# The second ff's up projection by pairs of column groups, with three of eight k-pairs as seven-for-eight block products

## The chip, the cores and the metric

One core of a Trainium2 chip runs the whole layer as one program. The metric is the device time of one execution in microseconds (us); the median of three runs is given. The engines are PE (TensorE: matmuls and transposes, results in eight PSUM banks, called PA and PB here, four of each), DVE (VectorE), ACT (ScalarE), POOL (GpSimd) and SP (SyncE, whose queue issues most loads).

## The reference, cut to what matters

The layer is a half-step SwiGLU, a token mixing (attention and Hyena groups), and a second half-step SwiGLU, each with a norm and a modulation in front. There are 256 latent tokens, D_MODEL is 2048 and D_FF is 5632. The change lies in the second SwiGLU:

```python
def swiglu(h, w_up, w_down):
    gate, up = jnp.split(h @ w_up, 2, axis=-1)
    return (jax.nn.silu(gate) * up) @ w_down

def half_ffn(s, m, slot, g, w_up, w_down):
    h = modulate(rms_norm(s, g), chunk(m, 3 * slot), chunk(m, 3 * slot + 1))
    return s + 0.5 * chunk(m, 3 * slot + 2) * swiglu(h, w_up, w_down)

x = half_ffn(x, mod, 2, g_norm[l, 2], w_ffn2_up[l], w_ffn2_down[l])
```

All arrays are f32. Here `h` is 256 x 2048 and `w_up` 2048 x 11264.

## The kernel before

Products are done in three passes on split numbers: a number is written as hi (rounded to the type fp32r) plus lo (the remainder), and hi x hi, hi x lo and lo x hi are added up in PSUM. `split_to` makes the two: a cast on ACT (`S.copy`), and a subtraction on DVE. `weight` does the same for a loaded weight tile of 128 x 1024: the load goes out on SP's queue into one of four `raw` buffers, the cast (L236) writes one of three `whi`, the remainder (L240) one of three `wlo`.

The up projection of the second ff runs over 22 groups `g`. A group is 512 columns: 256 gate columns and the 256 up columns that belong to them. For each of eight k-pairs `kp` (two of the 16 blocks of 128 along D_MODEL) one weight tile is prepared, and `tok_mm` (L1383 to L1385) multiplies: `h` is the stationary operand (128 x 128, one token tile), the weights are the moving one (512 columns); three passes for each of two token tiles and two k-blocks, 12 matmuls per weight tile. A group accumulates in two PA banks, one for each token tile. At its end ACT takes SiLU of the gate half (L1576) and DVE multiplies it with the up half (L1577). One group later, at `kp == 2`, `turn_act` transposes the product by PE into a PB bank (four transposes of 128 x 128, L1540) and splits it into two `act` tiles (L216, L217), which the down projection takes as stationary operands.

The down projection runs over four column blocks `b` of 512, each over 22 weight tiles. At the end of a block the result is multiplied by the gate row, added to the residual stream `xt[t][b]` and stored.

SBUF tiles of most kinds come from one pool `U` of 58 buffers of 128 x 512 f32: the 16 tiles of `h`, the eight tiles of `xt`, and those of the 44 `act` tiles that don't lie in the pool `fp` (which has EXTRA of them). The order of the instructions on each engine is made by a scheduler at build time from the data's dependences and its own estimates; `then(behind, ...)` (that is, `issue_after`) forces an instruction behind another on its engine. Waits are semaphores, also built in from the dependences, so an engine executes in its order and stands still at an instruction whose operand or buffer isn't ready.

Of the kernel before, what the change touches and what calls it, by code (L numbers as in the profile page):

```python
# [11 lines left out]
F32 = mybir.dt.float32  # L12
F32R = mybir.dt.float32r
AF = mybir.ActivationFunctionType
# [4 lines left out]
P = 128  # L19
D = 2048  # L20
KT = D // P
L = 256
# [5 lines left out]
NB = 4  # L28
UPG = FF // 256
# [18 lines left out]

AWAKE2 = 8

EXTRA = 14

KV_PLAN = ((0, 0, 1), (0, 0), (0, 0, 1), (0, 0, 1), (0, 1, 0), (1, 0), (1,), (1, 1))
KV_PLAN2 = (2, 1, 2, 1, 2, 1, 2, 1)
# [8 lines left out]
def hybrid_layer_kernel(ctx: ExitStack, tc: tile.TileContext, a):  # L63
    nc = tc.nc
    V, S, G, PE = nc.vector, nc.scalar, nc.gpsimd, nc.tensor
    serial = [0]

    def T(pool, shape, tag, dt=F32, bufs=None):
        serial[0] += 1
        kw = {} if bufs is None else {"bufs": bufs}  # L70
        return pool.tile(list(shape), dt, tag=tag, name=f"{tag}_{serial[0]}", **kw)

    const = ctx.enter_context(tc.tile_pool(name="const", bufs=1))
    wp = ctx.enter_context(tc.tile_pool(name="wp", bufs=3))
    up = ctx.enter_context(tc.tile_pool(name="up", bufs=1))
    pp = ctx.enter_context(tc.tile_pool(name="pp", bufs=4, space=PSUM))

    def U(shape, dt=F32):
        return T(up, shape, "u", dt, 58)
# [7 lines left out]
    def PA(shape=(P, 512)):  # L87
        return T(pp, shape, "pa")

    def PB(shape=(P, 512)):  # L90
        return T(pp, shape, "pb")
# [564 lines left out]
    dram = ctx.enter_context(tc.tile_pool(name="dram", bufs=1, space=bass.MemoryType.DRAM))  # L656
    spec = [T(dram, (P, 2, L), f"spec{i}") for i in range(8)]
    silu_rows = T(dram, (2, KT, P), "silu_rows")
    actd = [T(dram, (P, 2, 2, L), f"act{j}", F32R) for j in range(JT)]

    def filter_spectrum():
# [137 lines left out]
    for i in range(2):  # L799
        for q in range(KT // 2):  # L800
            t = U((P, 2, L))
# [6 lines left out]
    w = {j: tuple(T(wp, (P, 4, 2, P), n, F32R, 3) for n in ("whi", "wlo")) for j in range(WAVE)}  # L808
# [28 lines left out]
    sums = PB((P, 4, 2))  # L837
    awake = keep_awake(AWAKE[0])
    step, acc, summed = None, None, []
# [4 lines left out]
    for n, t in enumerate(xs[0] + xs[1]):  # L844
        i, sq = n // 8, U((P, 2, L))
# [5 lines left out]
        if n in (7, 14):  # L851
            sq = acc
# [11 lines left out]
        summed, last = [], awake  # L864
# [55 lines left out]
    made = then(roots[-1], first_hi, 0, head)  # L920
    for j in range(WAVE):
        made = then(made, first_hi, j, head) if j else made
# [3 lines left out]
    with tc.issue_after(scaled.ins):  # L926
        copied, turned_, bank = then(spread_last, ada_col, 0)
# [26 lines left out]
    with tc.issue_after(mm.ins), tc.issue_after(scaled.ins), tc.issue_after(shifted.ins):  # L954
        copied, mm, _ = ada_col(1)
# [4 lines left out]
    with tc.issue_after(shifted.ins), tc.issue_after(lo_last.ins):  # L960
        for j in range(2):
            first_lo(j, second)
        made = first_hi(2, second)
# [569 lines left out]
        shape = (P, 2, L)  # L1533
        return U(shape, F32R) if n >= EXTRA else T(fp, shape, "act", F32R, EXTRA)

    def turn_act(g, at):
        pt = PB((P, 2, L))
        for f in range(2):
            for t in range(2):
                PE.transpose(pt[:, f, t * P : (t + 1) * P], at[:, t, f * P : (f + 1) * P], ident)  # L1540
        acts.append(split_to(pt, act_tile(2 * g), act_tile(2 * g + 1)))

    prev = None
    for g in range(UPG):
        ps = [PA(), PA()]
        behind = None
        if g == 0:
            for t in range(2):
                for k in range(4):
                    tok_mm(ps, [h[k][:, s, :] for s in range(2)], ws[k], k == 0, False, (t,))  # L1550
                if t == 0:
                    pt = turned(xn)
                    for d in range(4):
                        hi, lo = mod2(d, pt[:, d, :], h[d][:, :, P:L])
                        behind = behind or (lo, hi)
            rest_h(1)
        for kp in range(8):
            if g == 0 and kp < 2:
                continue
            if g == 0 and kp == 2:  # L1560
                pieces = ws[4:6]
            else:
                late = dict(zip(("behind", "behind_hi"), behind)) if g == 0 and kp < 6 else {}
                whi, wlo = weight(a["w_up2"][g, kp], (P, 2, 512), **late)
                pieces = [(whi[:, k2, :], wlo[:, k2, :]) for k2 in range(2)]
            for k2 in range(2):
                k = 2 * kp + k2
                tok_mm(ps, [h[k][:, s, :] for s in range(2)], pieces[k2], k == 0, k == KT - 1)
            if g == 0 and kp in (2, 4):
                rest_h(kp // 2 + 1)  # L1570
            if kp == 2 and prev:
                turn_act(*prev)
        at = U((P, 2, L))
        for t in range(2):
            sg = tmp2((P, L))
            S.activation(sg, ps[t][:, 0:L], AF.Silu)  # L1576
            V.tensor_mul(at[:, t, :], ps[t][:, L : 2 * L], sg)  # L1577
        prev = (g, at)
    h = None
    for b in range(NB):  # L1580
        ps = [PA(), PA()]
        for fq in range(UPG):
            whi, wlo = weight(a["w_dn2"][b, fq], (P, 2, 512))
            if b == 0 and fq == UPG // 2:
                grow = gate_row(1)
            if b == 0 and fq == 2:
                turn_act(*prev)
            for t, f in ((0, 0), (1, 0), (0, 1), (1, 1)) if fq < UPG - 1 else ((0, 0), (0, 1), (1, 0), (1, 1)):
                tok_mm(ps, [t_[:, f, :] for t_ in acts[fq]], (whi[:, f, :], wlo[:, f, :]), fq + f == 0, fq == UPG - 1 and f == 1, (t,))
        for t in range(2):  # L1590
            o = tmp2((P, 512))
            V.tensor_mul(o, ps[t], grow[b])
            V.tensor_add(xt[t][b], xt[t][b], o)
            nc.sync.dma_start(a["out"][t, :, b * 512 : (b + 1) * 512], xt[t][b])
# [48 lines left out]
def _prepare(i):  # L1643
    i = {k: np.asarray(v) for k, v in i.items()}
    c_ = np.ascontiguousarray

    def pcol(v):
        return c_(v.reshape(-1, P).T)

    def pair(w, ncol):  # L1650
        return c_(w.reshape(4, 4, P, 2, ncol, P).transpose(4, 0, 2, 1, 3, 5))

    def wide(w):
        n = w.shape[1] // 256
        return c_(w.reshape(4, 4, P, n, 256).transpose(3, 0, 2, 1, 4)).reshape(n, 4, P, 4, 2, P)

    def down(w):
        return c_(w.reshape(JT // GRP, GRP, P, 8, 256).transpose(0, 3, 2, 1, 4)).reshape(JT // GRP, 8, P, GRP, 2, P)

    def cols(w):  # L1660
        return c_(w.reshape(8, 2, P, 512).transpose(0, 2, 1, 3))

    d = _constants()
    xc = np.concatenate([i["x"][0], i["ctx"][0]], axis=0)
    d["xT"] = c_(xc.reshape(2, L, KT // 2, 2, P).transpose(0, 2, 4, 3, 1))
    cc = np.stack([i["c"][0], i["c_ctx"]])
    d["crow"] = c_(cc)
    cs = cc.reshape(2, KT, P).transpose(2, 1, 0).reshape(P, 2, KT)
    wa = i["w_ada"][0]
    d["w_adaT"] = c_(wa.T).reshape(9 * KT, P, D)  # L1670
    blocks = [np.concatenate([wa[:, o + b * P : o + (b + 1) * P] for o in (D, 0)], axis=1) for b in range(KT)]
    d["w_ada1"] = np.stack([w.reshape(2, 8, P, 2 * P).transpose(0, 2, 1, 3) for w in blocks])
    gn = i["g_norm"][0].reshape(3, KT, P).transpose(2, 0, 1)
    d["cond"] = np.concatenate([pcol(i["b_ada"][0]).reshape(P, 9, KT), gn, cs], axis=1)
    w = pair(i["w_ffn1_up"][0], JT)
    d["w_up1"] = c_(w[:WAVE])
    w = w[WAVE:].reshape(JT - WAVE, 4, P, 2, 4, P)
    d["w_up1q"] = c_(w[:, :, :, :, [0, 2, 3, 1], :])
    d["w_dn1"] = down(i["w_ffn1_down"][0])
    w = i["w_ffn2_up"][0].reshape(8, 2, P, 2, UPG, 256)  # L1680
    d["w_up2"] = c_(w.transpose(4, 0, 2, 1, 3, 5)).reshape(UPG, 8, P, 2, 512)
    d["w_dn2"] = c_(i["w_ffn2_down"][0].reshape(UPG, 2, P, NB, 512).transpose(3, 0, 2, 1, 4))
    wi = i["w_in"][0]
    d["w_kv"] = cols(c_(wi[:, 1024:1536]))
    d["w_q"] = np.stack([cols(c_(wi[:, 0:512])), cols(c_(wi[:, 512:1024]))])
    d["w_hy"] = pair(np.concatenate([wi[:, 3584:4608], wi[:, 2560:3584]], axis=1), CT)
    d["w_x0"] = wide(c_(wi[:, 1536:2560]))
    d["w_o"] = np.stack([cols(c_(i["w_out"][0][:, b * 512 : (b + 1) * 512])) for b in range(NB)])

    def eo(v):  # L1690
        return np.concatenate([v[0::2], v[1::2]])

    d["qkg"] = np.stack([eo(i["q_norm"][0]), eo(i["k_norm"][0])])
    d["convw"] = c_(i["conv_w"][0].reshape(3, 3 * CT, P).transpose(2, 0, 1))
    d["convb"] = pcol(i["conv_b"][0])
    d["hyb"] = pcol(i["hy_bias"][0])
    d["gout"] = pcol(i["g_out"][0])
    w1, w2, w3, d["flt_w4"] = (c_(i[f"flt_w{n}"][0]) for n in (1, 2, 3, 4))
    head = np.zeros((P, 4, 64), np.float32)
    head[0:33, 0], head[0:64, 1], head[0:64, 2], head[0:64, 3] = w1, w2, w3, w3  # L1700
    vec = np.stack([i["flt_b1"][0], i["flt_b2"][0], i["flt_b3"][0], i["flt_freq"][0]], axis=1)
    d["flt_head"] = np.concatenate([head.reshape(P, 256), np.concatenate([vec, vec]), d.pop("tneg")], axis=1)
    d["flt_decay"] = c_(i["flt_decay"][0].reshape(1, 2 * HW))
    return d
# [19 lines left out]
```

## Time and profile before

| what | value |
|---|---|
| median of three runs | 2610.24 us (2609.64 to 2611.66) |
| the profiled execution's own time | 2610.55 us |
| its span in the profile | 2608.7 us |
| granted TensorE clock, mean | 0.998 |
| PE busy | 2587.4 us, 99% of the span, 14480 matmuls and transposes |
| DVE busy | 1895.7 us, 73%, 3051 instructions |
| ACT busy | 1103.9 us, 42%, 1543 instructions |
| HBM read, written | 544.05 MB, 38.57 MB |

The span goes from the first to the last instruction that the profiler saw; the execution's time has some 2 us more around it. "Busy" is the sum of the instructions' times on an engine. A wait is listed with what released it. The second ff's up projection begins at about 1870 us of the span and ends at about 2365 us; the down projection follows until the end.

### The profile page before, as it was taken

The page shows a single profiled execution, that of the slowest core. Times are in us where ns is not written, and L with a number is a line of the kernel's source. Part 1 is how long each engine was busy: PE and PEld are TensorE (multiplying, and loading weights), DVE is VectorE, ACT ScalarE, POOL GpSimd, SP SyncE. Part 2 cuts the span into 40 slices and gives each one's busy share as a digit, 9 for nine tenths or more (in the row PEclk, how much of TensorE's full clock was granted, in tenths as well). Part 3 has the DMA queues.
Part 4 walks back from the last instruction along what each step waited for, and adds up shares of the span by engine and source line. Part 5 has one row for each costly group of instructions (what it writes and reads, how often), then busy time and mean ns, then how long its engine had stood idle before and what let it go on. Part 6 is the DMA issues. An engine that isn't in the chain of part 4 may idle for free.

```text
span 2608.7 us, 37979 instructions
## 1 busy us (share of the span) xinstructions
PE 2587.4 (99%) x14480; PEld 2226.6 (85%) x14480; DVE 1895.7 (73%) x3051; ACT 1103.9 (42%) x1543; POOL 298.6 (11%) x475
## 2 busy tenths in 40 slices
PE   8999999999999999999999999999999999999999
PEld 5678999999999998888888988888788888888887
DVE  6776888888888887778988786888755454544444
ACT  5344444444444442112211565466544444444333
POOL 1122222222222223310010000000000000000000
PEclk9999999999999999999999999999999999999999
DMA  9987889889889889996897566335556665656664
GB/s 368 358 283 215 250 244 251 243 242 255 249 251 249 241 241 356 395 324 210 295 330 229 168 194 187 109 128 175 170 187 192 187 192 187 191 188 209 201 202 155
DMA packets 194275, 606.63 MB, mean 233 GB/s; under 512 B 22923, under 2 KB 25964, under 8 KB 189740
## 3 DMA queue, kind: packets, MB, share of 16 engines
q1 hardware_dynamic: 134396, 482.37, 56.0%
q0 software_dynamic: 59504, 121.70, 18.3%
q8 instruction: 113, 1.85, 0.3%
q14 instruction: 70, 0.57, 0.1%
q10 hardware_dynamic: 192, 0.13, 0.0%
HBM read 544.05 MB, written 38.57 MB: 223 GB/s over the span
## 4 chain that ended last, share of the span: by engine, by line
PE 95%; DMA 2%; DVE 1%; issue 1%; ACT 0%; SPq 0%; POOL 0%; POOLq 0%; DVEq 0%; ACTq 0%
PE pa L1384 10%; PE pa L1383 10%; PE pa L1385 10%; PE pb L247 9%; PE pb L248 9%; PE pb L249 9%; PE pa L247 9%; PE pa L248 9%; PE pa L249 9%; PE pa L255 3%; PE pa L257 2%; PE pa L1097 1%; PE pa L1098 1%; PE pa L1096 1%; DMA wrow<-in_w_ada_dram 1%
## 5 line engine op out<-in xcount | busy, mean ns | idle before, releaser
L240 DVE TENSOR_TENSOR wlo<-raw,whi 128x1024 fp32r<-128x1024 f32 x483 | 590.4, 1223 | 470.8 <-ACT whi L236 469.6
L236 ACT CAST whi<-raw 128x1024 fp32r<-128x1024 f32 x483 | 508.3, 1053 | 876.8 <-PE pa L1385 413.3
L1383 PE MATMUL pa<-whi,u 128*128 128x512 f32 x1060 | 413.9, 391 | 0.0
L1384 PE MATMUL pa<-wlo,u 128*128 128x512 f32 x1060 | 412.8, 390 | 0.2 <-DVE wlo L240 0.2
L1385 PE MATMUL pa<-whi,u 128*128 128x512 f32 x1060 | 412.9, 390 | 0.0
L247 PE MATMUL pa<-u,whi 128*128 128x256 f32 (+1 forms) x912 | 307.1, 337 | 2.1 <-ACT u L894 2.1
L248 PE MATMUL pa<-u,whi 128*128 128x256 f32 (+1 forms) x912 | 304.8, 334 | 0.4 <-DVE u L899 0.4
L249 PE MATMUL pa<-u,wlo 128*128 128x256 f32 (+1 forms) x912 | 304.5, 334 | 0.0
L247 PE MATMUL pb<-u,whi 128*128 128x256 f32 (+1 forms) x904 | 300.1, 332 | 0.0
L248 PE MATMUL pb<-u,whi 128*128 128x256 f32 (+1 forms) x904 | 298.5, 330 | 0.0
L249 PE MATMUL pb<-u,wlo 128*128 128x256 f32 (+1 forms) x904 | 298.4, 330 | 0.0
L1385 PEld LDWEIGHTS pa<-whi,u 128*128 128x128 f32 x1060 | 199.0, 188 | 41.6
L1384 PEld LDWEIGHTS pa<-wlo,u 128*128 128x128 f32 x1060 | 199.1, 188 | 41.3 <-DVE wlo L240 0.6
L1383 PEld LDWEIGHTS pa<-whi,u 128*128 128x128 f32 x1060 | 199.0, 188 | 40.7
L151 DVE CUSTOM_DVE_ANT_0 adas<-adaw,crow,cond 128x1024 bf16<-128x1024 f32 x160 | 204.8, 1280 | 13.0 <-DMA adaw<-in_w_adaT_dram 11.2
L151 DVE CUSTOM_DVE_ANT_0 adas<-adaw,crow,mod 128x1024 bf16<-128x1024 f32 x160 | 204.9, 1281 | 12.1 <-DMA adaw<-in_w_adaT_dram 10.1
L459 ACT CAST bhi<-raw 128x768 fp32r<-128x768 f32 x111 | 92.5, 833 | 268.6 <-PE pb L248 133.8
L247 PEld LDWEIGHTS pa<-u,whi 128*128 128x128 f32 x912 | 173.1, 190 | 24.7 <-issue 4.9
L248 PEld LDWEIGHTS pa<-u,whi 128*128 128x128 f32 x912 | 173.5, 190 | 17.5 <-DVE u L899 1.5
L249 PEld LDWEIGHTS pa<-u,wlo 128*128 128x128 f32 x912 | 173.5, 190 | 17.1
L247 PEld LDWEIGHTS pb<-u,whi 128*128 128x128 f32 x904 | 171.8, 190 | 17.0 <-issue 1.6
L248 PEld LDWEIGHTS pb<-u,whi 128*128 128x128 f32 x904 | 171.9, 190 | 16.3 <-issue 0.9
(361 smaller groups left out, 4817.5 us busy)
## 6 DMA issues: line engine op xcount, KB each, us to landing
adaw<-in_w_adaT_dram SPq DMA_DIRECT2D x224, 512.0 KB, 5.9
raw<-in_w_dn_dram SPq DMA_DIRECT2D x182, 512.0 KB, 4.4
raw<-in_w_up_dram SPq DMA_DIRECT2D x176, 512.0 KB, 3.5
raw<-in_w_up1q_dram SPq DMA_DIRECT2D x124, 512.0 KB, 5.1
u<-act POOLq DMA_DIRECT2D x136, 256.0 KB, 10.6
wrow<-in_w_ada_dram SPq DMA_DIRECT2D x32, 1024.0 KB, 9.3
act<-sg POOLq DMA_DIRECT2D x86, 256.0 KB, 6.3
plain<-in_w_up1q_dram POOLq DMA_DIRECT2D x80, 256.0 KB, 4.6
```

The lines of the kernel that those rows point to most:

```text
L151: V.tensor_tensor_reduce(out=sc, in0=t, in1=crow[i][:, b * (D // 2) : (b + 1) * (D // 2)], scale=1.0, scalar=mcol if b else bada[:, c * KT ...
L236: S.copy(hi, raw)
L240: last_lo[0] = V.tensor_sub(lo, raw, hi.bitcast(F32))
L247: PE.matmul(ps, w[0], xx[0], start=start, stop=False)
L248: PE.matmul(ps, w[0], xx[1], start=False, stop=False)
L249: return PE.matmul(ps, w[1], xx[0], start=False, stop=stop)
L255: PE.matmul(ps, w[0], x, start=start, stop=stop)
L257: PE.matmul(ps[:, 0, :], w[1], x[:, 0, :], start=False, stop=False)
L459: return raw, hi, lo, S.copy(hi, raw[:, :, 0:3])
L1383: PE.matmul(ps[t], hi, w[0], start=start, stop=False)
L1384: PE.matmul(ps[t], hi, w[1], start=False, stop=False)
L1385: last = PE.matmul(ps[t], lo, w[0], start=False, stop=stop)
```

## The change

Groups 0 and 1 stay as they were, but for two things: at `g == 0`, `kp == 5`, the residual stream's eight tiles are stored in DRAM by POOL's queue, and at `g == 1` the sums and differences of `h`'s blocks are made for three k-pairs (`combine`). The other 20 groups are done as ten pairs `p`. A pair accumulates in four banks (one for each token tile and group). For each k-pair, `quad` prepares both groups' weights one k-pair ahead.

In pairs 1 to 9 the k-pairs 2, 4 and 6 are "summed": the 2 x 2 blocks of `h` (two token tiles, two k-blocks) times the 2 x 2 blocks of weights (two k-blocks, two groups) are done by seven products of block sums instead of eight products of blocks. `quad` then makes the sums of the weights' blocks on DVE, in place in the raw buffers, and splits them; three of the seven products go into the pair's four banks directly, four go into four extra banks (`mixed`), which `collect` adds up into SBUF after k-pair 6; `gated` adds these to the pair's banks at the end. The prepared weights lie in five unit buffers: three in the pool `wp`, two in `fp`. All casts of the quads are issued in one order on ACT, and all sums and remainders in one order on DVE (`in_turn`).

Both groups of a pair are transposed at the next pair's k-pair 1. In the down projection the two tiles of the residual stream that a block needs are loaded back by POOL's queue. The weights of groups 2 to 21 come in another layout (`w_up2p`) with the same number of bytes.

```diff
-EXTRA = 14
+EXTRA = 9
+SUMMED = (2, 4, 6)
+SUM_PAIRS = range(1, 10)
...
+    xtd = [[T(dram, (P, 512), f"xt{t}_{b}") for b in range(NB)] for t in range(2)]
...
+    def combine(kp):
+        m_, s_ = tmp2((P, 2, L)), U((P, 4, P))
+        for n in range(2):
+            V.tensor_add(m_[:, n, :], h[2 * kp + n][:, 0, :].bitcast(F32), h[2 * kp + n][:, 1, :].bitcast(F32))
+        (a11, a21), (a12, a22) = ((m_[:, n, 0:P], m_[:, n, P:L]) for n in range(2))
+        V.tensor_add(s_[:, 0, :], a21, a22)
+        V.tensor_sub(s_[:, 1, :], s_[:, 0, :], a11)
+        V.tensor_sub(s_[:, 2, :], a11, a21)
+        V.tensor_sub(s_[:, 3, :], a12, s_[:, 1, :])
+        sums[kp] = split(s_, (P, 4, P))
...
+    def unit():
+        units[0] += 1
+        pool, tag, bufs = (wp, "w", 3) if units[0] % 5 < 3 else (fp, "v", 2)
+        return tuple(T(pool, (P, 2, 512), tag + name, F32R, bufs) for name in ("hi", "lo"))
+
+    def in_turn(engine, do, *args):
+        queue[engine] = then(queue[engine], do, *args) if engine in queue else do(*args)
...
+    def quad(p, kp):
+        raw = [weight_load(a["w_up2p"][p - 1, 2 * kp + k2], (P, 2, 512)) for k2 in range(2)]
+        if not summed(p, kp):
+            made = []
+            for k2 in range(2):
+                made.append(unit())
+                cast_in_turn(made[-1][0], raw[k2])
+                rest_in_turn(made[-1][1], raw[k2], made[-1][0])
+            return made
+        (b11, b12), (b21, b22) = ((r[:, 0, :], r[:, 1, :]) for r in raw)
+        first = tuple(T(up, (P, 512), "sq", F32R, 2) for _ in range(2))
+        plain, odd, even = unit(), unit(), unit()
+        cast_in_turn(first[0], b11)
+        cast_in_turn(plain[0], raw[1])
+        rest_in_turn(first[1], b11, first[0])
+        rest_in_turn(plain[1], raw[1], plain[0])
+        in_turn("dve", V.tensor_sub, b11, b12, b11)
+        in_turn("dve", V.tensor_sub, b12, b22, b12)
+        cast_in_turn(odd[0], raw[0])
+        in_turn("dve", V.tensor_sub, b22, b22, b11)
+        in_turn("dve", V.tensor_sub, b21, b21, b22)
+        rest_in_turn(odd[1], raw[0], odd[0])
+        cast_in_turn(even[0], raw[1])
+        rest_in_turn(even[1], raw[1], even[0])
+        return plain, first, odd, even
...
+    def multiply(p, kp, w, banks, mixed):
+        ks = [[h[2 * kp + k2][:, s_, :] for s_ in range(2)] for k2 in range(2)]
+        if not summed(p, kp):
+            for k2 in range(2):
+                for n in range(2):
+                    tok_mm([banks[t, n] for t in range(2)], ks[k2], halves(w[k2], n), kp + k2 == 0, kp == 7 and k2 == 1)
+            return
...
+        for bank, x, w_, inner in ((banks[0, 0], part(ks[1], 0), halves(plain, 0), True),
+                                   (banks[0, 1], part(both, 3), halves(plain, 1), True),
+                                   (mixed[0], part(ks[0], 0), first, False),
+                                   (mixed[3], part(both, 0), halves(odd, 0), False),
+                                   (mixed[2], part(both, 2), halves(odd, 1), False),
+                                   (banks[1, 0], part(ks[1], 1), halves(even, 0), True),
+                                   (mixed[1], part(both, 1), halves(even, 1), False)):
+            tok_mm([bank], x, w_, not inner and begin, not inner and end, (0,))
+
+    def collect(mixed):
+        e11, e21, e12, e22 = (U((P, 512)) for _ in range(4))
+        u2 = tmp2((P, 512))
+        S.copy(e11, mixed[0])
+        V.tensor_add(u2, e11, mixed[1])
+        V.tensor_add(e21, u2, mixed[2])
+        V.tensor_add(e12, u2, mixed[3])
+        V.tensor_add(e22, e21, mixed[3])
+        return {(0, 0): e11, (0, 1): e12, (1, 0): e21, (1, 1): e22}
+
+    def gated(p, banks, extra):
+        for n in range(2):
+            at = U((P, 2, L))
+            for t in range(2):
+                c_ = banks[t, n]
+                if extra:
+                    V.tensor_add(extra[t, n], extra[t, n], c_)
+                    c_ = extra[t, n]
+                sg = tmp2((P, L))
+                S.activation(sg, c_[:, 0:L], AF.Silu)
+                V.tensor_mul(at[:, t, :], c_[:, L : 2 * L], sg)
+            yield 2 * p + n, at
...
-    for g in range(UPG):
+    for g in range(2):
...
+            if g == 0 and kp == 5:
+                for t in range(2):
+                    for b in range(NB):
+                        nc.gpsimd.dma_start(xtd[t][b], xt[t][b])
+            if g == 1 and kp in (3, 4, 5):
+                combine(SUMMED[kp - 3])
...
+    plan = [(p, kp) for p in range(1, UPG // 2) for kp in range(8)]
+    ahead = quad(*plan[0])
+    turns = [prev]
+    for n, (p, kp) in enumerate(plan):
+        mine, other = (PB, PA) if p % 2 else (PA, PB)
+        if kp == 0:
+            banks = {(t, n_): mine() for n_ in range(2) for t in range(2)}
+            mixed = extra = None
+        if kp == SUMMED[0] and p in SUM_PAIRS:
+            mixed = [other() for _ in range(4)]
+        w = ahead
+        if n + 1 < len(plan):
+            ahead = quad(*plan[n + 1])
+        multiply(p, kp, w, banks, mixed)
+        if kp == 1:
+            for turn_ in turns:
+                turn_act(*turn_, other)
+        if kp == SUMMED[-1] and mixed:
+            extra = collect(mixed)
+        if kp == 7:
+            turns = list(gated(p, banks, extra))
+    h = sums = None
     for b in range(NB):
         ps = [PA(), PA()]
+        for t in range(2):
+            xt[t][b] = U((P, 512))
+            nc.gpsimd.dma_start(xt[t][b], xtd[t][b])
...
             if b == 0 and fq == 2:
-                turn_act(*prev)
+                for turn_ in turns:
+                    turn_act(*turn_)
```

`cast_in_turn` is `S.copy` and `rest_in_turn` is `V.tensor_sub` (raw less hi), both through `in_turn`; `summed(p, kp)` is true for the 27 summed k-pairs; `halves(w, n)` is group `n`'s half of a unit's hi and lo, and `part(x, n)` a token tile's half of an `h` tile, or one of the four made by `combine`.

More of the change, by code (lines that the diff above doesn't have):

```diff
@@ L1534, in act_tile, with turn_act @@
         return U(shape, F32R) if n >= EXTRA else T(fp, shape, "act", F32R, EXTRA)
-    def turn_act(g, at):
-        pt = PB((P, 2, L))
+    def turn_act(g, at, bank=PB):
+        pt = bank((P, 2, L))
         for f in range(2):
@@ L1541, in turn_act @@
         acts.append(split_to(pt, act_tile(2 * g), act_tile(2 * g + 1)))
+    sums = {}
+    def combine(kp):
[8 more added lines that the diff above has]
+        sums[kp] = split(s_, (P, 4, P))
@@ new lines, in hybrid_layer_kernel, with cast_in_turn, rest_in_turn @@
+    units = [0]
+    queue = {}
+    def unit():
[4 more added lines that the diff above has]
+        queue[engine] = then(queue[engine], do, *args) if engine in queue else do(*args)
+    def cast_in_turn(hi, raw):
+        in_turn("act", S.copy, hi, raw)
+    def rest_in_turn(lo, raw, hi):
+        in_turn("dve", V.tensor_sub, lo, raw, hi.bitcast(F32))
@@ new lines, in summed @@
+    def summed(p, kp):
+        return p in SUM_PAIRS and kp in SUMMED
+    def quad(p, kp):
[23 more added lines that the diff above has]
+        return plain, first, odd, even
@@ new lines, in halves, with part @@
+    def halves(w, n):
+        return [t[:, n, :] for t in w]
+    def multiply(p, kp, w, banks, mixed):
[5 more added lines that the diff above has]
+            return
+        plain, first, odd, even = w
+        def part(x, n):
+            return [t[:, n * P : (n + 1) * P] for t in x]
+        both = [t.rearrange("p a b -> p (a b)") for t in sums[kp]]
+        begin, end = kp == SUMMED[0], kp == SUMMED[-1]
+        for bank, x, w_, inner in ((banks[0, 0], part(ks[1], 0), halves(plain, 0), True),
[6 more added lines that the diff above has]
+            tok_mm([bank], x, w_, not inner and begin, not inner and end, (0,))
@@ L1578, in hybrid_layer_kernel @@
         prev = (g, at)
-    h = None
+    plan = [(p, kp) for p in range(1, UPG // 2) for kp in range(8)]
[20 more added lines that the diff above has]
+    h = sums = None
     for b in range(NB):
         ps = [PA(), PA()]
+        for t in range(2):
+            xt[t][b] = U((P, 512))
+            nc.gpsimd.dma_start(xt[t][b], xtd[t][b])
         for fq in range(UPG):
@@ L1680, in _prepare @@
     w = i["w_ffn2_up"][0].reshape(8, 2, P, 2, UPG, 256)
-    d["w_up2"] = c_(w.transpose(4, 0, 2, 1, 3, 5)).reshape(UPG, 8, P, 2, 512)
+    d["w_up2"] = c_(w.transpose(4, 0, 2, 1, 3, 5)[:2]).reshape(2, 8, P, 2, 512)
+    w = i["w_ffn2_up"][0].reshape(KT, P, 2, UPG // 2, 2, 256)
+    d["w_up2p"] = c_(w.transpose(3, 0, 1, 4, 2, 5)[1:]).reshape(UPG // 2 - 1, KT, P, 2, 512)
     d["w_dn2"] = c_(i["w_ffn2_down"][0].reshape(UPG, 2, P, NB, 512).transpose(3, 0, 2, 1, 4))
```

## The prediction

> **What bounds the kernel now.** I read the slices of the page first, then its chain, then the stage that is edited. The page:
>
> ```profile
> PE 2587.4 (99%) x14480; PEld 2226.6 (85%) x14480; DVE 1895.7 (73%) x3051; ACT 1103.9 (42%) x1543; POOL 298.6 (11%) x475
> DVE  6776888888888887778988786888755454544444
> PEclk9999999999999999999999999999999999999999
> PE 95%; DMA 2%; DVE 1%; issue 1%; ACT 0%; SPq 0%; POOL 0%; POOLq 0%; DVEq 0%; ACTq 0%
> ```
>
> PE is busy throughout and is 95% of the chain that ended last; DVE's digits fall to 5 and 4 in the last quarter, where the second ff lies. That stage by windows (stretch, length, busy us and count of PE, PEld, DVE, ACT, POOL, then clock, DMA share, GB/s), the second row being the down projection; then the first stretch's groups by form (line, engine, shapes, count, busy us, mean ns, idle before and its releaser):
>
> ```profile
> 1900.00:2300.00 400.00, 400.00 (x1800) 330.98 (x1799) 202.48 (x198) 171.83 (x199) 0.00 (x0) 1.00 0.61 190
> 2365.00:2603.00 238.00, 238.00 (x1054) 197.05 (x1053) 113.47 (x100) 90.38 (x87) 0.00 (x0) 1.00 0.63 194
> ```
>
> ```profile
> L240 DVE TENSOR_TENSOR wlo<-raw,whi 128x1024 fp32r<-128x1024 f32 x144 | 176.4, 1225 | 190.8 <-ACT whi L236 190.8
> L236 ACT CAST whi<-raw 128x1024 fp32r<-128x1024 f32 x145 | 152.6, 1052 | 206.5 <-PE pa L1385 206.5
> L1577 DVE TENSOR_TENSOR u<-pa,sg 128x256 f32<-128x256 f32 x36 | 15.3, 424 | 7.2 <-ACT sg L1576 4.6
> L1540 PE MATMUL pb<-ident,u 128*128 128x128 f32 x72 | 10.8, 272 | 0.0
> L217 DVE TENSOR_TENSOR act<-pb,act 128x512 fp32r<-128x512 f32 x7 | 4.8, 682 | 0.0
> ```
>
> Four hundred of 400 us are PE; DVE works 202 and waits for ACT's casts, which wait for PE to free a weight buffer. So this stage is bound by the number of matmuls, and DVE has about half its time free. A matmul's record overlaps its successor's, so its price is the distance of starts:
>
> ```profile
> 1893.81 0.39 PE L1383 MATMUL pa<-whi,u 128*128 128x512 f32 x1
> ...
> 1899.93 0.39 PE L1383 MATMUL pa<-whi,u 128*128 128x512 f32 x1
> ```
>
> There are 27 starts between these two: 6.12 / 27 = 0.2267 us per matmul. The period of a group, from ACT's SiLU to the same one a group later:
>
> ```profile
> 2007.28 0.38 ACT L1576 ACTIVATE sg<-pa 128x256 f32<-128x256 f32 x1 [0.98 <-PE pa L1385]
> 2029.53 0.38 ACT L1576 ACTIVATE sg<-pa 128x256 f32<-128x256 f32 x1 [0.98 <-PE pa L1385]
> ```
>
> That is 22.25 us: 96 x 0.2267 = 21.76, and 0.49 for four transposes (0.12 each). Two groups take 44.5 us.
>
> **The change, part by part.**
>
> *Matmuls (the gain).* Call a k-pair of two column groups a quad. A plain quad is 24 matmuls (2 k-tiles x 2 groups x 2 token tiles x 3 passes), 5.44 us; a summed one has seven products of three, 21 matmuls, 4.76 us. Summed are k-pairs 2, 4, 6 of pairs 1 to 9: 27 quads, 81 matmuls of an unchanged shape: 81 x 0.2267 = 18.4 us. The transposes stay the same in number. A summed pair of groups becomes 183 x 0.2267 + 8 x 0.12 = 42.5 us of PE.
>
> *DVE (the cost that must hide).* Its ops back to back:
>
> ```profile
> 1843.84 0.75 DVE L1406 SCALAR_TENSOR_TENSOR sg<-pa,small,u 128x512 f32<-128x512 f32 x1
> 1844.62 0.69 DVE L1407 TENSOR_TENSOR u<-u,sg 128x512 f32<-128x512 f32 x1
> 1845.23 0.74 DVE L1406 SCALAR_TENSOR_TENSOR sg<-pa,small,u 128x512 f32<-128x512 f32 x1
> 1845.89 1.21 DVE L240 TENSOR_TENSOR wlo<-raw,whi 128x1024 fp32r<-128x1024 f32 x1
> 1847.02 0.68 DVE L1407 TENSOR_TENSOR u<-u,sg 128x512 f32<-128x512 f32 x1
> 1847.62 0.68 DVE L217 TENSOR_TENSOR u<-raw,u 128x512 fp32r<-128x512 f32 x1
> 1848.23 1.22 DVE L240 TENSOR_TENSOR wlo<-raw,whi 128x1024 fp32r<-128x1024 f32 x1
> ```
>
> A 512-wide op costs 0.61 from start to start (1844.62 to 1845.23, 1847.62 to 1848.23) and a 1024-wide one 1.13 (1845.89 to 1847.02). An op that needs the one just before it starts 0.12 later (1843.84 to 1844.62 is 0.78, where the same op with an independent successor takes 0.66). A summed pair of groups now holds 10 remainders of plain units and 9 of summed ones (19 x 1.13 = 21.5); 512-wide: 15 in the summed quads (one remainder and four sums each), four in collect, four adds in gated, two in the turns (25 x 0.61 = 15.3); four gate products (4 x 0.42 = 1.7); some 11 dependent steps (1.3). Sum 39.8 us under PE's 42.5: DVE goes from under half to 94%, just below PE.
>
> The Trainium skill ("VectorE: DVE Perf Modes", section "The DRAIN you can't avoid") says that after an operation the next one doesn't start until the pipe is empty, and in the same breath that one which isn't held starts earlier. The rows above are of the second sort: successors start 0.08 us before the record ends.
>
> Without that overlap the same work is 19 x 1.225 + 25 x 0.69 + 4 x 0.424 = 42.2 us, level with PE; that is a rival below.
>
> *Does each summed quad arrive in time?* Five unit buffers serve 2 + 3 units, so a summed quad is prepared while the summed quad before it and the plain one between them run (4.76 + 5.44 = 10.20 us). ACT's half-size cast and the landings:
>
> ```profile
> L216 ACT CAST u<-raw 128x512 fp32r<-128x512 f32 x6 | 3.4, 614 | 0.4 <-DMA raw<-in_w_up_dram 0.4
> raw<-in_w_up_dram SPq DMA_DIRECT2D x176, 512.0 KB, 3.5
> raw<-in_w_up1q_dram SPq DMA_DIRECT2D x124, 512.0 KB, 5.1
> adaw<-in_w_adaT_dram SPq DMA_DIRECT2D x224, 512.0 KB, 5.9
> act<-sg POOLq DMA_DIRECT2D x86, 256.0 KB, 6.3
> u<-act POOLq DMA_DIRECT2D x136, 256.0 KB, 10.6
> ```
>
> Let k-pair 2's products start at 0. The small buffer ("first") comes free after the third product, 9 x 0.2267 + about 0.2 for the tail of the record = 2.24. Then: first cast to 2.85, plain cast to 3.9, plain remainder to 5.05, two sums to 6.3, the next two sums to 7.6 beside the odd cast, odd remainder to 8.75, even remainder to 9.9. Products of k-pair 4 start at 10.2 and want plain at once, odd at 12.24, even at 13.6: 5.1, 3.5 and 3.7 us early. For k-pair 6 the raw buffers are freed at 8.75 and 9.9 and the loads land 3.5 to 4 us later, so the plain cast starts at 13.9, the odd remainder ends at 19.8 and the even one at 20.95; wanted at 22.44 and 23.8. It is about 2.7 us early, the tightest place. The plain quad between (remainders at 9.9 to 11.1 and 11.5 to 12.6) is wanted from 14.96. Casts and remainders are issued in one order per engine (in_turn), so a late sum also holds the next quad's. After k-pair 6 come three plain quads in a row, and the slack is refilled. So I take zero for these waits; the bounds are 0 (nothing in this work can shorten PE) and 0.45 us per summed quad, i.e. 12 us, by the rows 5.1 and 5.9 for a landing (1.6 to 2.4 us more, just inside the 2.7) plus a cast queued wrongly ahead (1.05). If this cover goes, PE waits in the odd or even product, and every quad behind it moves.
>
> *Collect, gate, turns.* Collect: one copy and four adds, 0.6 + 4 x 0.61 + dependent steps = 3.3 us after k-pair 6; its banks are wanted at the next pair, 5.4 us later. Gated: four adds and four products, 4.1 us on DVE, at the next pair's k-pair 0; their banks are wanted after k-pair 1, 10.9 us on. What is queued behind these on DVE and ACT is the preparation of the next pair's quads. Before, that fits:
>
> ```profile
> 2006.33 1.23 DVE L240 TENSOR_TENSOR wlo<-raw,whi 128x1024 fp32r<-128x1024 f32 x1 [1.50 <-ACT whi L236]
> 2007.70 0.42 DVE L1577 TENSOR_TENSOR u<-pa,sg 128x256 f32<-128x256 f32 x1
> 2008.38 0.42 DVE L1577 TENSOR_TENSOR u<-pa,sg 128x256 f32<-128x256 f32 x1 [0.26 <-ACT sg L1576]
> 2009.31 1.23 DVE L240 TENSOR_TENSOR wlo<-raw,whi 128x1024 fp32r<-128x1024 f32 x1 [0.51 <-ACT whi L236]
> ```
>
> The gate takes the place where it becomes ready, between remainders of weights that are wanted later. I take 0; bounds 0 to 2 us per pair (18 us), half of the 4.1 us showing.
>
> *Combine*, three times in group 1. The nearest ops by size:
>
> ```profile
> L1453 DVE TENSOR_TENSOR u<-mt,u 128x256 fp32r<-128x256 f32 x12 | 4.5, 420 | 0.6 <-ACT u L1453 0.6
> L1453 DVE TENSOR_TENSOR u<-mt,u 128x128 fp32r<-128x128 f32 x6 | 1.5, 286 | 2.2 <-ACT u L1453 2.2
> ```
>
> Two 256-wide (0.42 each), four 128-wide (0.29), one remainder 0.68: 2.7 us each, 8 us in a group of 22 us where DVE is half idle; 0, at most 8. The start of pair 1 fills units in other buffers: I allow 1 us with this (0 to 3).
>
> *The residual stream.* Eight stores of 256 KB on POOL's queue, which is idle here (0.00 in the windows), and two loads per down block of 59.5 us (238 / 4). Landing by the rows 6.3 and 10.6 us, nobody waits. The 2.1 MB go beside weight loads at 190 GB/s and 0.61 share; the casts wait for PE, not for loads, in all 206.5 us. Zero; at most 2.1 MB / 0.31 MB per us (190 / 0.61 GB/s) = 6.7 us, were all of it in the weights' way. The freed buffers are taken up: in pair 9, 16 for h, 6 for the sums, 36 - 9 = 27 act tiles, 4 of collect and 2 products make 55 of 58, so no tile should wait for a buffer.
>
> **Sum.** The profiled execution took 2610.55 us (span 2608.7): 2610.55 - 18.4 + 1 = 2593.2. The median of the runs, 2610.24, lies 0.3 lower, so 2593.
>
> **Rivals.**
>
> 1. *Partial stalls* of 0.15 to 0.45 us per summed quad, at k-pair 6, where the slack is least: 4 to 12 us come back, 2597 to 2605. For it: 94% on DVE. Against: 2.7 us of slack.
>
> 2. *The pair's end eats the gain*: gate and collect stand ahead of the next quads' casts and remainders on in-order engines, and PE waits 2.04 us at each of nine pairs (18.4 / 9). Result about 2610, no change. For it: 4.1 us of gate where 0.85 stood, and k-pair 1 wants its remainders 5.4 us after the pair's end (4.1 + 2 x 1.13 = 6.4, already 1 us late if all of it went first). Against: the order in the rows above.
>
> 3. *Slower: DVE becomes the bound.* If ops don't overlap once each is held by a wait, a pair is 42.2 us of DVE, and each summed quad has hand-offs to ACT in which DVE stands idle (0.5 us ahead of the plain remainder in my schedule, more where a raw is late). From 2.3 us of idle per pair (44.5 - 42.2) the change loses; with 3.3 us it is 9 x 1.0 = 9 us more: 2619. For it: the chain of casts and sums is serial. Against: the overlaps shown, which hold also for L217 with its cast awaited.
>
> It is also what the section "The DRAIN you can't avoid" of the Trainium skill's "VectorE: DVE Perf Modes" would come to here, its first half taken at its word.
>
> **Chances.** Forecast 0.57 (its own range 2590 to 2597); rival 1 0.14; rival 2, within 0.2% (5.2 us, about what a measurement of this kernel tells from no change) 0.14; rival 3 and other slower ones, such as landings over 8 us (3.5 + 2.7 + 2.04), 0.15. Faster is 0.57 + 0.14 = 0.71. The range 2589 to 2609 takes the first two and most of the third, about 0.8; its low end is the sum without the 1 us (2592) less 0.1% for the measurement.
>
> **What would show it.** Right: 14,399 instructions on PE; a period of 42.5 us from pair to pair; DVE about 94% busy in pairs 1 to 9, and no PE wait on a remainder. DVE's busy time grows by 27 x (5 x 0.69 + 1.225) + 18 x 2.76 + 8 = 184 us to about 2080. Wrong: PE waits listed at the odd or even products (slack mis-sized), at k-pairs 0 and 1 (pair's end), or a DVE without gaps and a pair of 44.5 us or more (DVE the bound).

## The result, and the profile after

The changed kernel takes 2625.23 us (median of four runs, 2623.91 to 2627.84) against 2610.68 us for the kernel before in the same comparison: ratio 1.0057, 95% interval 1.0040 to 1.0074. The forecast was 2593. It is some 15 us slower where 18 less were expected, so about 32 us have to be found.

The page of the changed kernel, the lines that answer to those of before:

```profile
PE 2581.5 (98%) x14399; PEld 2212.3 (84%) x14399; DVE 2054.0 (78%) x3306; ACT 1148.9 (44%) x1609; POOL 307.3 (12%) x491
DVE  6777888888888886778988786888778888874444
PE 81%; DVE 8%; DMA 7%; ACT 3%; issue 1%; ACTq 0%; SPq 0%; DVEq 0%
```

The 81 instructions are gone from PE (14480 to 14399), and yet PE holds only 81% of the chain that ended last, 95% before: DVE, DMA and ACT have come into it. The stretch from the transposes of pair 3 to those of pair 10, seven pairs long, as windows (stretch, length, busy us and count of PE, PEld, DVE, ACT, POOL, clock, DMA share, GB/s):

```profile
2022.90:2345.18 322.28, 304.88 (x1338) 244.45 (x1337) 276.25 (x335) 168.69 (x204) 1.08 (x2) 1.00 0.56 185
```

A pair takes 322.28 / 7 = 46.04 us: 42.5 were forecast, and 44.5 is two groups of before. PE is no longer full (304.88 of 322.28), nor is DVE (276.25, 86%), nor ACT, nor the DMA engines (0.56). No engine is saturated, so the loss has to lie in what waits for what. PE's stops from pair 4's second quad to the end of its summed ones, out of its timeline (L1386 to L1388 are the three passes of `tok_mm`, L1543 the transposes, L219 the remainder of a turned product; L272 is the helper that forces an order, so there the tiles tell what an operation is: `whi` and `wlo`, `vhi` and `vlo` are units, `sq` is the first block, and `raw` a sum in place):

```profile
2064.46 0.50 PE L1387 MATMUL pa<-wlo,u 128*128 128x512 f32 x1 [1.01 <-DVE wlo L272]
2069.82 1.03 PE L1543 MATMUL pb<-ident,u 128*128 128x128 f32 x8
2074.58 0.50 PE L1386 MATMUL pb<-vhi,u 128*128 128x512 f32 x1 [0.99 <-DVE u L219]
2095.41 0.49 PE L1386 MATMUL pb<-vhi,u 128*128 128x512 f32 x1 [0.38 <-ACT vhi L272]
2096.83 0.50 PE L1387 MATMUL pb<-vlo,u 128*128 128x512 f32 x1 [0.93 <-DVE vlo L272]
```

PE stops at k-pair 2's fifth product (2074.58), which waits for DVE to split the turned products and free a bank, and at k-pair 6's fourth (2095.41 and 2096.83), which waits for the odd unit's cast and remainder. Every pair from 3 to 9 shows these two, and some a stop at a plain quad (2064.46). What those waits stand on is told by the chain that ended last in this stretch (start, us, what):

```profile
2072.82 4.80 DMA raw<-in_w_up2p_dram
...
2077.69 1.06 ACT whi L272
...
2078.78 1.22 DVE wlo L272
2080.00 0.61 DVE raw L272
...
2080.64 0.70 DVE raw L272
...
2081.36 0.70 DVE raw L272
...
2082.09 0.70 DVE raw L272
...
2083.17 1.06 ACT vhi L272
...
2084.25 1.24 DVE vlo L272
2085.51 4.97 DMA raw<-in_w_up2p_dram
```

No PE stands in it. It is one round of one raw buffer: a load, the plain cast, the plain remainder, four sums in place (each waits for its predecessor), the even cast, the even remainder, and only then is the buffer free for the next load, 12.69 us later (2072.82 to 2085.51). Four raw buffers hold the loads of two quads, so a round has to serve one summed and one plain quad, 10.20 us of products.

The round begins late, too. Ahead of it, at the pair's end, the same chain lies on DVE for most of 11.8 us (2060.98 to 2072.82):

```profile
2059.58 1.05 ACT whi L272
...
2060.98 0.42 DVE u L1658
2061.41 0.60 DVE u L1654
...
2066.48 1.14 DVE wlo L272
...
2071.57 1.24 DVE vlo L272
```

These are the gate's adds (L1654) and products (L1658) among the remainders, then k-pair 2's sums and remainders; the last of them frees the buffer for the load at 2072.82.

### The profile page after: what moved, and what is told of

It is laid out like the page before. It is cut to its first block, busy times and chain, and to the rows that moved or that the text cites. A ratio compares the mean times of both kernels' runs of the same rounds, so it can differ in the third digit from the quotient of the medians.

```text
span 2624.4 us, 38215 instructions
## 1 busy us (share of the span) xinstructions
PE 2581.5 (98%) x14399; PEld 2212.3 (84%) x14399; DVE 2054.0 (78%) x3306; ACT 1148.9 (44%) x1609; POOL 307.3 (12%) x491
## 4 chain that ended last, share of the span: by engine, by line
PE 81%; DVE 8%; DMA 7%; ACT 3%; issue 1%; ACTq 0%; SPq 0%; DVEq 0%
PE pb L249 9%; PE pb L250 9%; PE pb L251 9%; PE pa L249 9%; PE pa L250 9%; PE pa L251 9%; DMA raw<-in_w_up2p_dram 5%; PE pa L1387 5%; PE pa L1388 5%; PE pa L1386 5%; PE pa L257 3%; DVE raw L272 3%; DVE wlo L272 2%; PE pa L259 2%; ACT whi L272 1%; DVE vlo L272 1%
## 5 line engine op out<-in xcount | busy, mean ns | idle before, releaser
L238 ACT CAST whi<-raw 128x1024 fp32r<-128x1024 f32 x323 | 339.9, 1053 | 649.0 <-PE pb L250 191.5
L242 DVE TENSOR_TENSOR wlo<-raw,whi 128x1024 fp32r<-128x1024 f32 x323 | 394.4, 1222 | 259.5 <-ACT whi L238 258.4
L1388 PE MATMUL pa<-whi,u 128*128 128x512 f32 x656 | 255.6, 390 | 0.0
L1387 PE MATMUL pa<-wlo,u 128*128 128x512 f32 x640 | 250.3, 391 | 4.7 <-DVE wlo L272 4.1
L1386 PE MATMUL pa<-whi,u 128*128 128x512 f32 x640 | 250.1, 392 | 3.2 <-DVE u L219 1.9
L251 PEld LDWEIGHTS pb<-u,wlo 128*128 128x128 f32 x904 | 171.9, 190 | 15.6
L464 DVE TENSOR_TENSOR blo<-raw,bhi 128x768 fp32r<-128x768 f32 x111 | 106.2, 956 | 95.5 <-ACT bhi L461 95.4
L272 ACT CAST whi<-raw 128x1024 fp32r<-128x1024 f32 x115 | 118.8, 1051 | 105.6 <-DVE raw L272 47.9
```

The costliest lines, as they stand in the source:

```text
L238: S.copy(hi, raw)
L242: last_lo[0] = V.tensor_sub(lo, raw, hi.bitcast(F32))
L251: return PE.matmul(ps, w[1], xx[0], start=False, stop=stop)
L272: return do(*args, **kw)
L464: return V.tensor_sub(lo, raw[:, :, 0:3], hi.bitcast(F32))
L1386: PE.matmul(ps[t], hi, w[0], start=start, stop=False)
```

## The experiments

Theory A: four raw buffers are too few for such a round, since a load can be asked for only when the quad two before has been prepared. Theory B: DVE's amount of work, and its hand-offs with ACT, set the pace. Theory C: the turned products' split stands in the wrong place of DVE's queue. Theory D: the structure by pairs costs by itself. Times of before in the same comparisons were 2610.7 to 2610.9 us.

**Without the sums (e1).**

```diff
-SUM_PAIRS = range(1, 10)
+SUM_PAIRS = ()
```

> SUM_PAIRS is empty, all else as in the changed kernel: pairs of groups, four banks, quads one ahead, the residual stream in DRAM; no seven-for-eight products, no sums, no collect. If the loss comes from how the summed quads are prepared (theory A, raw buffers, or B, DVE), PE goes without a stop: 2112 products again, so 2609 to 2613 us. If the pair structure itself costs (theory D: gate of four banks, two groups turned together, residual stores beside the loads), 2616 us or more.

Measured: 2610.12 us, ratio 1.0000 (0.9990 to 1.0009). Theory D falls: the four banks, the gate of four (without the adds of the sums), the two turns at once and the residual stream's way through DRAM cost nothing that can be measured. The loss is in the summed quads.

**A fifth raw buffer (e2).** `raws` counts the quads' loads; every fifth goes to a buffer in `fp`.

```diff
-EXTRA = 9
+EXTRA = 7
...
+    def quad_load(src):
+        raws[0] += 1
+        if raws[0] % 5 < 4:
+            return weight_load(src, (P, 2, 512))
+        raw = T(fp, (P, 2, 512), "more", bufs=1)
+        nc.sync.dma_start(raw, src)
+        return raw
...
-        raw = [weight_load(a["w_up2p"][p - 1, 2 * kp + k2], (P, 2, 512)) for k2 in range(2)]
+        raw = [quad_load(a["w_up2p"][p - 1, 2 * kp + k2]) for k2 in range(2)]
```

> A fifth raw buffer for the quads, in the place of two act tiles (EXTRA 7). Theory A: the round of one raw buffer (load 4.9, cast 1.06, remainder 1.22, four sums 2.85, cast 1.06, remainder 1.24 = about 12.4 us) for each 10.2 us of products is what is late; with five buffers a load is asked for one tile earlier, most of the 2.2 us of lateness goes: 2600 to 2612 us. Theory B: DVE's own work and order set the pace, a load that lands earlier changes nothing: 2622 to 2628 us.

Measured: 2592.92 us, ratio 0.9935 (0.9921 to 0.9950): below the range I gave theory A, and what the prediction had said of the change itself. The windows of the same seven pairs:

```profile
2014.05:2310.79 296.74, 296.74 (x1339) 246.15 (x1337) 276.08 (x333) 168.33 (x202) 1.08 (x2) 1.00 0.61 205
```

PE is full again, and a pair takes 42.39 us. With five buffers a round may last as long as five tiles' products in place of four, by the same count 10.20 x 5 / 4 = 12.75 us (an estimate). DVE does the same 276 us of work in less time (93%), with the same hand-offs to ACT. So neither is the bound, and theory B falls. In this stretch PE's matmuls have no wait at all. ACT's longest waits are now for the sums, which lie off PE's path; the casts that follow a load wait for PE once more, for instance the small one:

```profile
ACT sq L272 <- PE pa L1387: 5.6, 8, 0.7
```

(eight times, 5.6 us in total, in the list of waits). That is the order of things the prediction drew; in the changed kernel the same cast waits for a load:

```profile
ACT sq L272 <- DMA raw<-in_w_up2p_dram: 21.1, 19, 1.8
```

**The other half of that edit (e5).** Only EXTRA 7.

> The other half of the edit with five buffers, by itself: EXTRA 7 and four raw buffers, so that two act tiles more lie in the common pool. Theory A (the raw buffers alone): as the changed kernel, 2621 to 2629 us. If the place of the act tiles had made the gain: 2592 to 2600 us.

Measured: 2622.53 us, ratio 1.0044 (1.0029 to 1.0059). The place of the act tiles makes some 3 of the 32 us, and its interval overlaps the changed kernel's; the buffer makes the gain.

**The sums taken out of the round (e7).** This kernel leaves out the four sums of the weights' blocks, so its summed quads don't multiply what the layer asks for. In their place four subtractions of the same size on other data stand behind the quad's last remainder.

```diff
-        in_turn("dve", V.tensor_sub, b11, b12, b11)
-        in_turn("dve", V.tensor_sub, b12, b22, b12)
...
-        in_turn("dve", V.tensor_sub, b22, b22, b11)
-        in_turn("dve", V.tensor_sub, b21, b21, b22)
...
         rest_in_turn(even[1], raw[1], even[0])
+        aside = tmp2((P, 512))
+        for _ in range(4):
+            in_turn("dve", V.tensor_sub, aside, *[h[n].rearrange("p a b -> p (a b)").bitcast(F32) for n in range(2)])
```

> Four raw buffers; the four sums of each summed quad are left out, and four subtractions of the same size on other data (two h tiles into a scratch tile) are issued behind the quad's last remainder: the same number of DVE operations, none of them between a load and the raw buffer's release. Theory A: the round is 12.5 - 2.85 = 9.7 us, under 10.2: 2592 to 2605 us. Theory B (DVE's total of work): 2620 to 2628 us, as before the edit.

Measured: 2592.09 us, ratio 0.9927 (0.9910 to 0.9943), with four raw buffers and an unchanged number of DVE operations. PE has no stop in the pairs here either. The fifth buffer gave the round more time; this edit makes the round shorter (9.7 us by the sum above), and the time is the same. By itself e7 changes two things, since the odd and even casts no longer wait for sums; e2 kept those waits and lost the stops as well. Theory A holds; B is out.

**Another order, and the loads swapped (e3).**

```diff
-        raw = [weight_load(a["w_up2p"][p - 1, 2 * kp + k2], (P, 2, 512)) for k2 in range(2)]
+        raw = [None, None]
+        for k2 in (1, 0) if summed(p, kp) else (0, 1):
+            raw[k2] = weight_load(a["w_up2p"][p - 1, 2 * kp + k2], (P, 2, 512))
...
         rest_in_turn(first[1], b11, first[0])
-        rest_in_turn(plain[1], raw[1], plain[0])
         in_turn("dve", V.tensor_sub, b11, b12, b11)
         in_turn("dve", V.tensor_sub, b12, b22, b12)
+        rest_in_turn(plain[1], raw[1], plain[0])
```

> The same work in another order, four raw buffers: in a summed quad the second k-block's load goes first, and the two sums that need no remainder are made ahead of the plain remainder. Theory A: the round gets shorter by two sums and by one remainder's wait, 12.4 to about 9.9 us, below the 10.2 us of products, so the stops at k-pair 6 go (1.65 us per pair, 15 us in all): 2603 to 2613 us. Theory B (DVE's total of 39 us per pair and its hand-offs): same work, 2620 to 2628 us.

Measured: 2633.08 us, ratio 1.0081 (1.0066 to 1.0096), slower still. I had worked out its round wrongly. With the loads swapped, the first block lands last, and the whole order hangs on it, since its small cast is the first in the queue. The chain of this kernel:

```profile
2076.20 4.60 DMA raw<-in_w_up2p_dram
...
2080.88 0.63 ACT sq L272
...
2081.54 0.70 DVE sq L272
...
2088.72 4.33 DMA raw<-in_w_up2p_dram
```

The round is 12.52 us (2076.20 to 2088.72), not 9.9: what the sums no longer add behind the load, the small cast and its remainder do, and two sums stand ahead of the plain remainder, which PE wants first:

```profile
2097.12 0.50 PE L1387 MATMUL pa<-wlo,u 128*128 128x512 f32 x1 [1.17 <-DVE wlo L272]
```

The result misses both ranges and speaks neither for B nor against A; the edit didn't do what it was for.

**The order alone (e6).** The second half of that diff without the swap.

> The order of e3 without its change of the loads: the first k-block's load goes first again, and the small cast, its remainder and one sum are done while the second one still lands. Theory A: from the later landing the round is 4.9 + cast 1.06 + remainder 1.2 + two sums 1.4 + cast 1.06 + remainder 1.24 = 10.9 us in place of 12.5, near to the 10.2 us of products: most of the stops at k-pair 6 go, 2603 to 2614 us. Theory B (DVE's amount of work): 2622 to 2630 us.

Measured: 2613.37 us, ratio 1.0009 (1.0000 to 1.0019), 12 us below the changed kernel, at the upper end of theory A's range. The stops at k-pair 6 are gone. One per pair is left, at k-pair 2. PE's stop, and DVE's queue ahead of the split that it waits for:

```profile
2070.33 0.50 PE L1386 MATMUL pb<-vhi,u 128*128 128x512 f32 x1 [1.86 <-DVE u L219]
```

```profile
2067.32 2.35 DVE L272 TENSOR_TENSOR wlo<-raw,whi 128x1024 fp32r<-128x1024 f32 x2
2069.59 1.28 DVE L219 TENSOR_TENSOR u<-pb,u 128x512 fp32r<-128x512 f32 x2
```

**The turns' split in the quads' order: with the change's own order (e4), and with e6's (e9).**

```diff
-        acts.append(split_to(pt, act_tile(2 * g), act_tile(2 * g + 1)))
+        hi, lo = act_tile(2 * g), act_tile(2 * g + 1)
+        cast_in_turn(hi, pt)
+        rest_in_turn(lo, pt, hi)
+        acts.append((hi, lo))
```

(for the turns inside the pairs only)

> The split of the turned products goes into the quads' order, ahead of the next plain quad's remainders. Theory C: the stop at k-pair 2's fifth product (about 1.17 us per pair, it waits for this split to free its bank) is a loss of its own: 10 us come back, 2613 to 2617 us. Theory A: that stop only takes part of a lateness that the raw buffers set, and PE waits the longer at k-pair 4 and 6: 2621 to 2627 us.

> Four raw buffers, the order of e6 and the turns' split in the quads' order as in e4. What is left in e6 is one stop per pair, at k-pair 2's fifth product (0.5 to 1.9 us, behind two remainders of 1.13 us that stand ahead of the split on DVE). Theory C for this kernel (with the raw buffers' round near 10.2 us, that place in the queue is a loss of its own): it goes, 2594 to 2604 us. Theory A alone (the stop only takes up lateness from the raw buffers, and another stop replaces it): 2609 us or more.

Measured: e4 2621.54 us, ratio 1.0039 (1.0024 to 1.0054), inside theory A's range; e9 2611.76 us, ratio 1.0005 (0.9995 to 1.0015). Theory C falls twice. The stop at the fifth product goes or shrinks, and others take its place; in e9 mostly at the start of the next pair's k-pair 1:

```profile
2057.23 0.50 PE L1387 MATMUL pa<-wlo,u 128*128 128x512 f32 x1 [1.60 <-DVE wlo L272]
2101.44 0.50 PE L1387 MATMUL pb<-vlo,u 128*128 128x512 f32 x1 [1.25 <-DVE vlo L272]
```

The round in e9 is 10.77 us, still above 10.20, by two loads of its chain:

```profile
2076.47 4.48 DMA raw<-in_w_up2p_dram
...
2087.24 4.38 DMA raw<-in_w_up2p_dram
```

**Five buffers and the new order (e8).** e2 with e6's order.

> Five raw buffers (EXTRA 7) and the order of e6 together. In e2 PE has no stop left in the pairs, so theory A leaves nothing to gain: 2591 to 2595 us, as e2. Below 2590 us there would be a loss in e2 that its waits don't show.

Measured: 2593.64 us, ratio 0.9935 (0.9920 to 0.9950), the same as e2. In e2 PE has no stop left in the pairs, and the new order gains nothing on top. e2 and e8 beat both kernels, 2593 us against 2611 and 2625.

## Why the prediction was wrong, point by point

*The gain* was right: 81 matmuls less, and a pair of 42.39 us where PE doesn't stop (e2; 42.5 forecast). *DVE's work* was right too: 276 / 7 = 39.4 us per pair against 39.8, and at 93% it hides under PE (e2). Rival 3 didn't come as it was drawn: a pair took more than 44.5 us, but with DVE at 86% and not without gaps. The overlap of successive DVE operations that its sum rests on is borne out: the exception in the Trainium skill's section "The DRAIN you can't avoid" ("VectorE: DVE Perf Modes") is the case here, not its first half. Two remainders of 1.22 us each take 2.35 us together (2067.32 in e6). The forecast of DVE's busy time over the whole span missed: 184 us more were forecast, and 158 came (2054.0 less 1895.7). It had added records at full length; with 0.61 and 1.13 from start to start the same sum gives some 165. *Gate, collect, combine, residual stream* cost nothing that can be seen in e1 and e2. In the changed kernel the gate stands on the chain at the pair's end, a price that the prediction took as zero and named only in its bound and in rival 2.

*The step that failed* is "Does each summed quad arrive in time?", and in it three things, all about the raw buffers.

First, the schedule started with k-pair 2's products at 0 and took k-pair 4's weights as already there: plain cast from 2.85 to 3.9. Nothing in the text worked out when k-pair 2's own preparation ends and frees the buffers. Pair 4's transposes begin at 2069.82 and its k-pair 2 at about 2070.6; the next load on the chain goes out at 2072.82, behind the DVE work at the pair's end, and the plain cast of k-pair 4 starts at 2077.69, 7.1 us after the start in place of 2.85. That alone is 4.2 us, and the slack I had written down was 2.7 to 5.1.

Second, the landing. The row of 3.5 us is for loads that go out some 2.7 us apart. The same loads in the stretch 1960 to 2300 of four kernels (before, changed, e1, e2; in each the median in us stands last):

```profile
raw<-in_w_up_dram SPq DMA_DIRECT2D x123, 512.0 KB, 3.5
```

```profile
raw<-in_w_up2p_dram SPq DMA_DIRECT2D x116, 512.0 KB, 4.7
```

```profile
raw<-in_w_up2p_dram SPq DMA_DIRECT2D x123, 512.0 KB, 3.6
```

```profile
raw<-in_w_up2p_dram SPq DMA_DIRECT2D x103, 512.0 KB, 4.8
```

A summed quad frees its two buffers 1.3 us apart (loads at 2071.55 and 2072.82), and the plain quad behind it follows at once (2073.95, 2076.32), so the loads go out in runs. Taken one by one, the changed kernel's loads of this stretch that went out 3 us or more after the one before landed in 3.56 us (median of 22), those that followed within 1.5 us in 4.93 (median of 67). I had 3.5 to 4, and kept 5.1 and 5.9 for the end of the range. In e2 the landings are as long, and PE doesn't stop: they cost time only where the round has no room.

Third, the round itself. I followed the steps once from 0 to 20.95 and compared each with its due time, but never set the length of one full round against the products it has to cover. By my own numbers it was 3.5 to 4 + 1.05 + 1.15 + 2.5 + 1.1 + 1.2, that is 10.5 to 11 us against 10.2: over it already, with a slack that each round uses up. In that schedule one round takes the odd unit's slack from 3.5 us at k-pair 4 to 2.7 at k-pair 6, so this alone would not have stopped PE. Measured the round is 12.69: the landing was 4.80 in place of 3.5 to 4, and the sums took 2.8 in place of 2.5, as each waited for the one before (0.72 us from start to start, 2080.64 to 2081.36).

*The price.* PE's stops cost 46.04 - 42.39 = 3.65 us per pair, 33 us in nine, or 1.2 us per summed quad; I had taken zero, with a bound of 0.45. Rival 1 had the place (k-pair 6) and at most a third of the size, and the sign named for it, waits at the odd product, is what came. Rival 2's place, the pair's end and the turns, showed as well, but as a follower: mended in e4 and e9, its stop moved elsewhere.

The Trainium skill ("Perfetto Trace Analysis", section "Optimization Strategy") says that the same gap coming again and again on the engine that should be full can mean too few buffers for the next tile. The stops of 0.9 to 1.3 us at the same two products of each of pairs 3 to 9 are such a gap, and one buffer more removes them all.

*What stays open.* Why loads a little over 1 us apart land 1.4 us later, at less DMA traffic overall (183 GB/s against 189 before, in the stretch 1960 to 2300), wasn't measured by itself; that they share the engines is the plain reading, and not shown. How much of the loss DVE's work at the pair's end makes by itself wasn't measured either. That the slack of five buffers holds with other landings wasn't tried.

## What to carry to other kernels

When a change makes the preparation of a tile longer, close the circle: add up load, casts, in-place work and release for one buffer, divide by the number of tiles in flight, and compare that with the time their consumer needs, before looking at any engine's share of busy time. An in-place operation on a load buffer is part of that circle, even where its engine has room on average (the four sums are 2.8 us of the 12.69; e7, with the same number of operations but none of them in the circle, is 33 us faster than the changed kernel). And a stop that moves when its immediate cause is mended (e4, e9) can be a follower; look for the chain that doesn't contain the engine that stops.

## What the runs showed of the hardware that was not expected

The landing time of a 512 KB load went with how the loads are spaced: 3.5 to 3.6 us where they go out some 2.7 us apart (before, e1) and 4.7 to 4.8 where they go out in runs (changed, e2), at mean rates of 183 to 199 GB/s in all four. A stop costs PE more than the idle time that the trace gives: in the row at 2064.46 the idle is 1.01 us, yet the matmul before it started at 2063.06, so 1.40 lie between starts where 0.23 are usual, a loss of 1.17.

```profile
2063.06 0.39 PE L1386 MATMUL pa<-whi,u 128*128 128x512 f32 x1
```
